# A hybrid decoder layer on one core: orders of VectorE, GpSimd and LayerNorm work in the projection and the MLP, and later places for GLA's and RG-LRU's matmuls

## Chip, core and metric

The kernel runs on one core of a Trainium2 chip. The metric is the device time of one execution in microseconds. TensorE multiplies matrices (PE in the rows), VectorE (DVE), ScalarE (ACT) and GpSimd (POOL) work element by element, and SyncE (SP) issues the DMAs. Each engine has a list of instructions of its own and takes it strictly in order; an instruction whose input or buffer isn't ready holds up everything behind it in that list. Engines are joined by semaphores.

## What is computed

One post-LayerNorm decoder layer over 2048 tokens of width 1024, in float32:

```python
def _layer_norm(x, g, b):  # mean and variance over the 1024 columns, eps 1e-5
    ...
# each layer:
z   = h @ w_in                       # one projection, its columns shared among three mixers
#   S5     : diagonal complex state space, 16 groups x 16 channels, GLU (width 256)
#   GLA    : gated linear attention in chunks of 64, 4 heads (width 512)
#   RG-LRU : causal convolution of width 4, gates, a real linear recurrence (width 256)
mix = concat(S5, GLA, RG-LRU) @ w_out
h   = LayerNorm(alpha * h + mix)
h   = LayerNorm(alpha * h + relu(h @ mlp_w1)^2 @ mlp_w2)   # hidden width 4096
```

Ahead of the layer the input goes through a LayerNorm too.

## The kernel before

**Products.** Every float32 product is done as three TensorE matmuls of rounded halves (`mm3`, L226 to L228), so a weight or activation has to be split into a high and a low half first: ScalarE copies the rounded half, VectorE subtracts it (`split`, L1373 and the helper line L75). All VectorE and GpSimd instructions are recorded on L75, since they go through a counting wrapper there.

**Stages.** From 0 to about 680 us the input projection and the three mixers; to about 890 us the output projection with LayerNorm 1 and the transposes of its result; to about 1545 us the first MLP product; to about 2235 us the second; and a tail with LayerNorm 2.

**How the order is made.** The program writes each engine's list itself. Up to the output projection there is a plan of ticks, each a group of some 12 or 24 matmuls; in each tick `step()` is called twice and moves every generator in `active` on to its next `yield`. So a `yield` puts what follows half a tick later in every engine's list. One GLA unit (`gla_unit`) is such a generator: it makes decayed queries and keys (`gla_qz`, `gla_kz`) on VectorE, then the scores (`gps`) and a transpose of the keys (`kt`), the state update (`up`), the states (`gs`, VectorE), the output (`ov`) and its transpose (`ot`). `lru_work` is one generator over 8 units: convolution (`xc`), two gate products (`lps`), then sigmoids, scan and output. Besides, `filler` and other generators are taken on while the cost counted for VectorE or GpSimd in the tick is under a budget.

**Output projection.** `out_tile(i, dh)` makes one half of a 128-token tile (`po`) and adds it to the residual `acc`. `ln1_work` is one generator that takes the 16 tiles one after another, `tj_work` one that transposes the finished rows in 32 groups of four 128x128 blocks (`tjp`, PSUM), empties each into a `tjo` tile of seven operands of a fast matrix product (two copies by ScalarE, two differences by VectorE, two by GpSimd, two buffers) and stores it to `rop_d`. The first MLP product loads these operands back as `act` and `ring` pieces.

**MLP.** Both products use a Strassen-Winograd scheme: seven products p1, p2, p7, p6, p3, p4, p5 (`ORDER`) in three PSUM banks a, b, c. The first has 32 steps of seven products of 12 matmuls, the second 64 parts of seven products of 6. `run` goes through all of them with a counter n, one per product; p3 of a step is done in the next step at its place. Besides the products, each position n has a list of tasks put there by number: `task(n, fn)`. What is left of the transposes and the ring pieces when the first product begins is done by `tail_step`, two half-steps at each of the positions 0 to 10. `steps[n].hsum` makes the squared hidden activations out of the products. `Chunk` loads and adds up blocks of w2 (`load`, `sum`, `split`); `Part.evac` adds the seven products onto the quarters c11, c12, c21, c22 of an accumulator `accq`, on VectorE straight out of PSUM (`pa_m`, `pb_m`, `pc_m`), on GpSimd out of copies that ScalarE made (`p_m`, `u_m`, three rotating buffers of `pu_tile`). In the last eight parts `Acc.ln` and `Acc.ln_apply` do LayerNorm 2 of the two rows of a tile: statistics on VectorE, a power on GpSimd, then scale on ScalarE, the gain product on VectorE and the shift half on VectorE, half on GpSimd (`gb`).

## Time and profile before

| | us |
|---|---|
| median of three runs | 2258.49 |
| the three runs | 2260.07, 2258.49, 2255.2 |
| the profiled execution, as reported | 2259.39 |
| its span, first to last instruction | 2257.7 |

The profile is of one execution. A wait is idle time of an engine right ahead of an instruction, put down to what ended last of what it waited for. The granted clock is that of TensorE as a share of its full speed, averaged over a stretch. Matmuls are pipelined: one of 512 columns is shown as 0.39 us, while the next starts 0.227 us later.

### The profile page before, as it was taken

The numbers are of one execution on the slowest core, as the hardware profiler recorded it, in microseconds if no ns is written. First come the engines' busy times: TensorE is split into PE (matmuls) and PEld (weight loads), VectorE is DVE, ScalarE is ACT, GpSimd is POOL, SyncE is SP. The second block draws the span as 40 slices with busy tenths as digits, with TensorE's granted clock in tenths as the row PEclk, the third lists the DMA queues.
The fourth block names the chain that finished last, engine by engine and source line by source line (L and its number), as shares of the span: only waits on it lengthen the run. The fifth ranks groups of instructions, "written<-read, shape, count | busy, mean of one in ns | idle before, by whom it ended". The sixth has DMA issues, their size and how long they took to land. (4 is left out here: it accounts for less than half of the span.)

```text
span 2257.7 us, 29781 instructions
## 1 busy us (share of the span) xinstructions
PE 2067.0 (92%) x9920; PEld 1712.9 (76%) x9920; DVE 1584.5 (70%) x2262; ACT 1027.0 (45%) x2045; POOL 1147.3 (51%) x1087
## 2 busy tenths in 40 slices
PE   6977999899999998799999999998999999999863
PEld 6866779888987776588887888886788888888652
DVE  6567865546547556677778877776688888888887
ACT  3336655657663222333334433334544545444431
POOL 5486630000003444466666666666566675667554
PEclk9998999999999999899999999999999999999976
DMA  7342354455354676544447444437544344434332
GB/s 212 102 129 74 98 167 137 121 138 140 99 177 131 175 232 204 146 150 153 150 154 256 151 153 154 148 128 266 185 131 135 94 134 131 135 98 134 111 105 77
DMA packets 378457, 328.24 MB, mean 145 GB/s; under 512 B 72240, under 2 KB 314560, under 8 KB 378304
## 3 DMA queue, kind: packets, MB, share of 16 engines
q1 hardware_dynamic: 377536, 324.24, 46.5%
q0 software_dynamic: 768, 2.11, 0.4%
q8 instruction: 78, 1.28, 0.2%
q14 instruction: 75, 0.61, 0.1%
HBM read 208.23 MB, written 118.63 MB: 145 GB/s over the span
## 5 line engine op out<-in xcount | busy, mean ns | idle before, releaser
L75 DVE TENSOR_TENSOR ho_m<-ho_m 128x512 fp32r<-128x512 f32 (+1 forms) x256 | 259.3, 1038 | 68.2 <-ACT ho_m L1373 55.9
L75 POOL TENSOR_TENSOR accq<-accq,p_m 128x512 f32<-128x512 f32 x128 | 199.9, 1579 | 200.4 <-DVE accq L75 155.9
L75 POOL TENSOR_TENSOR cp<-cp,cp 128x512 f32<-128x512 f32 x128 | 196.0, 1540 | 183.2 <-ACT cp L1562 180.6
L75 DVE TENSOR_TENSOR w1o_s<-w_s,w1o_s 128x512 fp32r<-128x512 f32 x160 | 208.6, 1318 | 46.6 <-ACT w1o_s L1373 46.5
L75 POOL TENSOR_TENSOR ss<-ss,cst 128x4 f32<-128x4 f32 x16 | 17.6, 1102 | 365.8 <-DVE ss L75 365.8
L227 PE MATMUL pa_m<-act,ho_m 128*128 128x512 f32 x384 | 150.4, 392 | 2.0 <-DVE act L75 1.9
L226 PE MATMUL pa_m<-act,ho_m 128*128 128x512 f32 x384 | 150.3, 391 | 2.0 <-ACT p_m L1792 1.4
L228 PE MATMUL pa_m<-act,ho_m 128*128 128x512 f32 x384 | 150.1, 391 | 1.2 <-DVE ho_m L75 1.2
L1373 ACT ACTIVATE ho_m<-ho_m 128x512 fp32r<-128x512 f32 (+1 forms) x256 | 135.6, 569 | 30.7 <-DMA ho_m<-hid_d 30.7
L1373 ACT ACTIVATE w1o_s<-w_s 128x512 fp32r<-128x512 f32 x160 | 99.9, 626 | 103.1 <-PE pb_s L228 51.8
L1792 ACT ACTIVATE p_m<-pa_m 128x512 f32<-128x512 f32 x64 | 38.3, 599 | 221.7 <-PE pa_m L228 216.0
L226 PE MATMUL pa_s<-ring,w1o_s 128*128 128x512 f32 x256 | 103.0, 402 | 11.0 <-ACT ring L1373 6.3
L226 PE MATMUL pc_m<-act,ho_m 128*128 128x512 f32 x256 | 102.4, 400 | 5.5 <-ACT p_m L1792 5.4
L226 PE MATMUL po<-act,w_mx 128*128 128x512 f32 x256 | 106.9, 418 | 0.1
L75 POOL TENSOR_TENSOR accq<-accq,u_m 128x512 f32<-128x512 f32 x64 | 106.2, 1659 | 0.6 <-ACT u_m L1792 0.6
L75 DVE SCALAR_TENSOR_TENSOR cp<-cp 128x512 f32<-128x512 f32 x96 | 101.9, 1061 | 3.3
L227 PE MATMUL pa_s<-ring,w1o_s 128*128 128x512 f32 x256 | 102.2, 399 | 1.9 <-DVE ring L75 1.9
L228 PE MATMUL po<-act,w_mx 128*128 128x512 f32 x256 | 103.2, 403 | 0.9 <-DVE w_mx L75 0.9
L227 PE MATMUL pc_s<-act,w1o_s 128*128 128x512 f32 x256 | 101.4, 396 | 1.8 <-DVE act L75 1.8
L227 PE MATMUL po<-act,w_mx 128*128 128x512 f32 x256 | 102.8, 402 | 0.0
L226 PE MATMUL pc_s<-act,w1o_s 128*128 128x512 f32 x256 | 102.6, 401 | 0.0
L228 PE MATMUL pc_m<-act,ho_m 128*128 128x512 f32 x256 | 101.5, 397 | 0.5 <-DVE ho_m L75 0.5
(437 smaller groups left out, 6553.3 us busy)
## 6 DMA issues: line engine op xcount, KB each, us to landing
hid_d<-cp SPq DMA_DIRECT2D x224, 256.0 KB, 2.3
ho_m<-hid_d SPq DMA_DIRECT2D x384, 128.0 KB, 2.3
w_s<-in_mlp_w_dram SPq DMA_DIRECT2D x32, 1024.0 KB, 5.7
w<-in_mlp_w_dram SPq DMA_DIRECT2D x16, 1024.0 KB, 7.0
rop_d<-tjo SPq DMA_DIRECT2D x32, 448.0 KB, 4.6
w<-s5w_d SPq DMA_DIRECT2D x16, 640.0 KB, 5.1
xr<-in_x_dram SPq DMA_DIRECT2D x16, 512.0 KB, 4.9
h_d<-xr SPq DMA_DIRECT2D x16, 512.0 KB, 4.4
```

What stands on the lines that cost most here:

```text
L75: return fn(*a, **k)
L226: T.matmul(ps, lhs[0], rhs[0], start=first, stop=False, skip_group_check=more)
L227: T.matmul(ps, lhs[0], rhs[1], start=False, stop=False, skip_group_check=more)
L228: T.matmul(ps, lhs[1], rhs[0], start=False, stop=last, skip_group_check=more)
L1373: S.activation(dst_hi, src, COPY)
L1792: S.activation(t, ps, COPY)
```

## The change

Five places.

1. RG-LRU's generator yields twice more at the end of a unit, GLA's twice more between the keys and the scores and once more ahead of the output.
2. LayerNorm 1 is one generator for each tile, put into `active` when the tile's second half is added, in place of one generator over all. A transpose group takes one more half-step, and each pair of rows waits for both.
3. First MLP product: `tail_step` goes to position 17, the last ring piece is split two half-steps later, p3 of step 0 is done in step 2 just ahead of p7, and the tasks that hang on it move along (`hsum`, one split).
4. First chunk of w2: its first half is loaded five positions earlier and its two first sums are made half by half, from position L0 on in place of L0 + 2. In `evac`, GpSimd adds u2 behind VectorE's p4 and p7 behind VectorE's p5, in place of ahead of them; the copies stay where they were.
5. LayerNorm 2: row 1 at position 10 and row 0 at 13 in place of 0 at 13 and 1 at 14, each applied two positions later in place of two and three.

```diff
@@ lru_work, end of a unit
                     late.append(bind(mix_store, 6 + ct, b * BLK, gi))
+                    yield
+                    yield
@@ gla_unit, ahead of gps; ahead of ov
-        for _ in range(3):
+        for _ in range(5):
             yield
...
         gstate[hp] = st
+        yield
         yield
@@ out_tile, ln1_work, tj_work
             if dh:
-                z["acc", i] = True
+                active.append(ln1_work(i))
...
             if j == 0:
+                while ("row", 2 * g) not in z:
+                    yield
                 yield
                 yield
...
                 late.append(bind(z.__setitem__, ("tj", g), True))
+            yield
             yield
@@ run
-                who = prev if p == "p3" else g
...
+                if p != "p3":
+                    who = [(g, p)]
+                    if at_ == 2 and p == "p7":
+                        who.insert(0, (groups[0], "p3"))
+                else:
+                    who = [(groups[at_ - 1], p)] if at_ > 1 else []
@@ tail and tasks of the first product
-        for _ in range(4):
+        for _ in range(6):
             yield
...
-    for n in range(11):
+    for n in range(18):
         task(n, tail_step)
         task(n, tail_step)
...
-        for w, k in ((1, 5), (3, 6), (2, 6), (4, 7)):
+        for w, k in ((1, 10), (3, 10), (2, 11), (4, 11)) if n == 0 else ((1, 5), (3, 6), (2, 6), (4, 7)):
@@ Part.evac
             elif p == "p7":
-                self.add("c22", G, self.copy(bank["c"], "p7"))
+                self.p7 = self.copy(bank["c"], "p7")
             elif p == "p6":
-                self.add("c21", G, self.copy(bank["a"], "u2"))
+                self.u2 = self.copy(bank["a"], "u2")
             elif p == "p4":
                 self.add("c21", V, bank["c"])
+                self.add("c21", G, self.u2)
             elif p == "p5":
                 self.add("c22", V, bank["a"])
+                self.add("c22", G, self.p7)
@@ first chunk of w2; LayerNorm 2
-    task(L0, chunks[0].load)
-    for k, w in ((2, 3), (3, 1), (4, 2), (6, 4)):
+    task(L0 - 5, chunks[0].load, 0)
+    task(L0, chunks[0].load, 1)
+    for k, w, j in ((0, 3, 0), (1, 1, 0), (2, 3, 1), (3, 1, 1)):
+        task(L0 + k, chunks[0].sum, w, (j,))
+    for k, w in ((4, 2), (6, 4)):
         task(L0 + k, chunks[0].sum, w)
...
-        for i, k in ((0, 13), (1, 14)):
+        for i, k in ((1, 10), (0, 13)):
             task(n + k, acc[g].ln, i)
-            task(n + k + 2 + i, acc[g].ln_apply, i)
+            task(n + k + 2, acc[g].ln_apply, i)
```

ScalarE's list in the mixers, where the gate of a GLA unit (`gc`), the convolution of an RG-LRU unit (`xc`) and the copy of a projected RG-LRU gate (`lg`) meet. Before:

```order
L782 ACTIVATE gc_0_0_1969<-gc_0_0_1969 128x256
L783 ACTIVATE gc_0_0_1969<-gc_0_0_1969,cst 128x256
L724 ACTIVATE xc_0_1982<-xl_0_1921,lcb,lcw 128x512
L1024 ACT_TABLE_LOAD
L1024 ACTIVATE lg_0_2006<-pz_lg_1_1944 128x512
L791 ACT_TABLE_LOAD
```

And now:

```order
L784 ACTIVATE gc_0_0_1970<-gc_0_0_1970 128x256
L785 ACTIVATE gc_0_0_1970<-gc_0_0_1970,cst 128x256
L1027 ACT_TABLE_LOAD
L1027 ACTIVATE lg_0_2002<-pz_lg_1_1949 128x512
L793 ACT_TABLE_LOAD
L793 ACTIVATE gc_0_0_1970<-ga_0_0_1968 128x256
L794 ACTIVATE gd_0_0_1971<-ga_0_0_1968 128x256
L795 ACTIVATE gb_0_0_1969<-gb_0_0_1969 128x256
L797 ACTIVATE dec_0_0_2013<-ga_0_0_1968 128x4
L724 ACTIVATE xc_0_2020<-xl_0_1926,lcb,lcw 128x512
```

`xc` of the next RG-LRU unit stood ahead of `lg` and now stands behind it and behind the four exponentials of the GLA gate.

VectorE's list at the start of the first MLP product, around the last LayerNorm row (the two `acc_8204` operations), the weight splits (`w1o_s`) and the emptying of a transpose group (`tjo`). Before:

```order
L75 TENSOR_TENSOR tjo_8578<-tjp_8556,tjo_8578 128x128
L75 TENSOR_TENSOR tjo_8578<-tjo_8578,tjp_8556 128x128
L75 SCALAR_TENSOR_TENSOR acc_8204<-acc_8204,mv_ln_15_8541,g_ln_6662 128x640
L75 TENSOR_TENSOR w1o_s_5_8595<-s_s_7810,w1o_s_5_8595 128x512
L75 TENSOR_TENSOR act<-act 128x2x512 x2
L75 TENSOR_TENSOR w1o_s_0_8607<-w_s_7924,w1o_s_0_8607 128x512
L75 TENSOR_TENSOR w1o_s_1_8610<-w_s_7924,w1o_s_1_8610 128x512
L75 TENSOR_TENSOR w1o_s_2_8614<-w_s_7924,w1o_s_2_8614 128x512
L75 SCALAR_TENSOR_TENSOR acc_8204<-acc_8204,rs_ln_15_8543,b_ln_6663 128x640
L75 TENSOR_TENSOR tjo_8632<-tjp_8590,tjo_8632 128x128
L75 TENSOR_TENSOR tjo_8632<-tjo_8632,tjp_8590 128x128
```

And now:

```order
L75 SCALAR_TENSOR_TENSOR acc_8204<-acc_8204,mv_ln_15_8513,g_ln_6652 128x640
L75 TENSOR_TENSOR cp_8573<-pb_s_8528,p_s_8541 128x512
L75 SCALAR_TENSOR_TENSOR cp_8573<-cp_8573 128x512
L75 SCALAR_TENSOR_TENSOR acc_8204<-acc_8204,rs_ln_15_8515,b_ln_6653 128x640
L75 TENSOR_TENSOR w1o_s_5_8584<-s_s_7805,w1o_s_5_8584 128x512
L75 TENSOR_TENSOR act<-act 128x2x512 x2
L75 TENSOR_TENSOR w1o_s_0_8596<-w_s_7921,w1o_s_0_8596 128x512
L75 TENSOR_TENSOR w1o_s_1_8599<-w_s_7921,w1o_s_1_8599 128x512
L75 TENSOR_TENSOR w1o_s_2_8603<-w_s_7921,w1o_s_2_8603 128x512
L75 TENSOR_TENSOR tjo_8620<-tjp_8579,tjo_8620 128x128
L75 TENSOR_TENSOR tjo_8620<-tjo_8620,tjp_8579 128x128
```

The second half of the LayerNorm row stood behind the splits of `w1o_s` 5, 0, 1 and 2 and now stands ahead of them; the emptying of the group that followed it stands right behind the splits.

VectorE's list in the tail, one part: the first `pc_m` addition is c21 of a part, the statistics (`BN_STATS` to the short `rs`) are a LayerNorm row, `ho_m` are splits for the next part, `gb` the gain product and the shift. Before, from c21 of one part on:

```order
L75 TENSOR_TENSOR accq_13324<-accq_13324,pc_m_18268 128x512
L75 BN_STATS st_1_0_18333<-accq_13194 128x6 x2
L75 BN_AGGR mv_1_0_18336<-st_1_0_18333 128x2
L75 TENSOR_SCALAR rs_1_0_18338<-mv_1_0_18336 128x1
L75 SCALAR_TENSOR_TENSOR rs_1_0_18338<-mv_1_0_18336,rs_1_0_18338 128x1
L75 TENSOR_TENSOR accq_13324<-accq_13324,pa_m_18234 128x512
L75 BN_STATS st_1_1_18350<-accq_13194 128x6 x2
L75 BN_AGGR mv_1_1_18353<-st_1_1_18350 128x2
L75 TENSOR_SCALAR rs_1_1_18355<-mv_1_1_18353 128x1
L75 SCALAR_TENSOR_TENSOR rs_1_1_18355<-mv_1_1_18353,rs_1_1_18355 128x1
L75 TENSOR_TENSOR ho_m_0_18281<-ho_m_0_18281 128x512
L75 TENSOR_TENSOR accq_13194<-accq_13194,gb_18163 128x1024
```

And now:

```order
L75 TENSOR_TENSOR accq_13324<-accq_13324,pc_m_18274 128x512
L75 BN_STATS st_1_0_18347<-accq_13195 128x6 x2
L75 BN_AGGR mv_1_0_18350<-st_1_0_18347 128x2
L75 TENSOR_SCALAR rs_1_0_18352<-mv_1_0_18350 128x1
L75 SCALAR_TENSOR_TENSOR rs_1_0_18352<-mv_1_0_18350,rs_1_0_18352 128x1
L75 TENSOR_TENSOR accq_13324<-accq_13324,pa_m_18248 128x512
L75 TENSOR_TENSOR ho_m_0_18287<-ho_m_0_18287 128x512
L75 TENSOR_TENSOR accq_13195<-accq_13195,gb_18163 128x1024
L75 TENSOR_TENSOR accq_13195<-accq_13195,gb_18163 128x512
L75 TENSOR_TENSOR accq_13324<-accq_13324,pb_m_18365 128x512
L75 TENSOR_TENSOR ho_m_3_18327<-ho_m_3_18327 128x256
L75 TENSOR_TENSOR ho_m_1_18317<-ho_m_1_18317 128x512
```

The second row's statistics (`st_1_1`) followed on the first's with one addition between; now one row's statistics stand behind c21, and the next tile's other row (`st_2_1`) follows only after a split, the gain product, the shift, an addition and two splits.

## Rows read from the trace of the kernel before

**Rows 1.** The page: busy us (share of the span) and instructions of each engine
```profile
PE 2067.0 (92%) x9920; PEld 1712.9 (76%) x9920; DVE 1584.5 (70%) x2262; ACT 1027.0 (45%) x2045; POOL 1147.3 (51%) x1087
```

**Rows 2.** TensorE's waits, whole span: us in total, times, longest
```profile
PE pa_m L226 <- DVE accq L75: 44.1, 14, 9.7
...
PE gps L810 <- DVE gla_kz L75: 9.3, 5, 2.8
...
PE ov L842 <- DVE gs L75: 7.3, 1, 7.3
PE pr_v L226 <- ACT lg L1024: 6.4, 1, 6.4
...
PE lps L732 <- DVE xc L75: 2.9, 1, 2.9
```

**Rows 3.** Stretches: length, busy us (instructions) of PE, PEld, DVE, ACT, POOL; clock
```profile
60.00:300.00 240.00, 202.64 (x1105) 169.05 (x1104) 165.97 (x324) 124.37 (x279) 158.44 (x331) 0.92 0.37 107
...
690.00:890.00 200.00, 180.79 (x834) 146.56 (x832) 123.25 (x229) 55.30 (x138) 92.55 (x126) 0.96 0.62 188
890.00:960.00 70.00, 51.09 (x193) 39.83 (x194) 45.60 (x60) 26.07 (x51) 35.20 (x37) 0.80 0.56 168
...
1610.00:2105.00 495.00, 492.31 (x2165) 405.78 (x2165) 408.78 (x500) 238.04 (x457) 318.32 (x207) 1.00 0.41 122
2105.00:2258.00 153.00, 89.84 (x332) 69.74 (x331) 123.37 (x182) 46.95 (x70) 75.43 (x56) 0.78 0.31 97
```

**Rows 4.** ScalarE, timeline around lg: start, us, instruction, idle before
```profile
188.01 0.51 ACT L783 ACTIVATE gc<-gc,cst 128x256 f32<-128x256 f32 x1
191.68 0.81 ACT L724 ACTIVATE xc<-xl,lcb,lcw 128x512 f32<-128x512 f32 x1 [3.16 <-DVE lgi L75]
...
193.93 0.60 ACT L1024 ACTIVATE lg<-pz_lg 128x512 f32<-128x512 f32 x1
```

**Rows 5.** VectorE, timeline in the first GLA unit
```profile
126.05 1.28 DVE L75 SCALAR_TENSOR_TENSOR xr<-xr,rs_in,b_in 128x1024 f32<-128x1024 f32 x1 [6.70 <-POOL rs_in L75]
...
130.33 0.28 DVE L75 COPY gs<-up 128x128 f32<-128x128 f32 x1
```

**Rows 6.** Waits from 690 to 890 us, of TensorE and of ScalarE
```profile
PE tjp L1320 <- DVE tjo L75: 11.6, 6, 3.9
PE tjp L1320 <- DVE acc L75: 4.4, 2, 4.1
...
ACT tjo L1324 <- DMA rop_d<-tjo: 52.0, 9, 6.8
```

**Rows 7.** TensorE's waits from 890 to 960 us
```profile
PE tjp L1320 <- DVE tjo L75: 8.9, 1, 8.9
PE pa_s L226 <- ACT ring L1373: 6.3, 1, 6.3
PE pa_s L226 <- DVE tjo L75: 4.7, 1, 4.7
```

**Rows 8.** ScalarE, timeline at the last ring piece
```profile
943.41 1.06 ACT L1373 ACTIVATE ring<-ring 128x1024 fp32r<-128x1024 f32 x1 [5.40 <-DMA ring<-rop_d]
```

**Rows 9.** GpSimd, timeline at the first chunk of w2; then a stretch
```profile
1533.86 1.29 POOL L75 TENSOR_TENSOR t<-w 128x512 f32<-128x512 f32 x1 [8.00 <-DMA w<-in_mlp_w_dram]
...
1540.00:1556.00 16.00, 10.42 (x36) 6.26 (x34) 15.96 (x12) 11.76 (x21) 15.38 (x10) 0.95 0.63 206
```

**Rows 10.** VectorE, timeline of the tail
```profile
2141.22 0.69 DVE L75 TENSOR_TENSOR accq<-accq,pc_m 128x512 f32<-128x512 f32 x1 [0.56 <-POOL accq L75]
...
2191.45 1.78 DVE L75 TENSOR_TENSOR ho_m<-ho_m 128x512 fp32r<-128x512 f32 x1
...
2200.65 0.69 DVE L75 TENSOR_TENSOR ho_m<-ho_m 128x512 fp32r<-128x512 f32 x1
...
2228.03 0.69 DVE L75 TENSOR_TENSOR accq<-accq,pc_m 128x512 f32<-128x512 f32 x1 [1.78 <-POOL accq L75]
```

**Rows 11.** The page, costliest groups: busy, mean ns, idle before and releaser
```profile
L75 POOL TENSOR_TENSOR accq<-accq,u_m 128x512 f32<-128x512 f32 x64 | 106.2, 1659 | 0.6 <-ACT u_m L1792 0.6
```

More of the change, by code (lines that the diff above doesn't have):

```diff
@@ L1286, in out_tile, with ln1_work @@
             tick([un], bind(pe, h, un), ev if h else None)
-    def ln1_work():
-        for i in range(NT):
-            while ("acc", i) not in z:
-                yield
-            g = ln_steps(accs[i], z["gb1"], f"ln1_{i}", 384)
-            next(g)
-            yield
-            yield
-            yield
-            for _ in g:
-                yield
-            late.append(bind(lambda i: store(h1_d[i * P:i * P + P, :], accs[i]), i))
-            yield
-            z["row", i] = True
+    def ln1_work(i):
+        g = ln_steps(accs[i], z["gb1"], f"ln1_{i}", 384)
+        next(g)
+        yield
+        yield
+        yield
+        for _ in g:
+            yield
+        late.append(bind(lambda i: store(h1_d[i * P:i * P + P, :], accs[i]), i))
+        z["row", i] = True
     def set_gb(key, g_ap, b_ap, nm):
@@ L1313, in tj_work @@
             if j == 0:
+                while ("row", 2 * g) not in z:
+                    yield
                 yield
@@ L1333, in tj_work @@
                 late.append(bind(z.__setitem__, ("tj", g), True))
+            yield
             yield
@@ L1438, in evac @@
             last = None
-        for g in groups:
+        for at_, g in enumerate(groups):
             for p in ORDER:
-                who = prev if p == "p3" else g
-                if who is not None:
-                    products(who, p)
-                evac()
-                if who is not None:
-                    last = who, p
+                if p != "p3":
[4 more added lines that the diff above has]
+                    who = [(groups[at_ - 1], p)] if at_ > 1 else []
+                for w in who:
+                    products(*w)
+                    evac()
+                    last = w
+                if not who:
+                    evac()
                 for e in tasks.pop(n, ()):
@@ L1647, in hymba_layer_kernel @@
         task(b + max(2, o), m.sum, 4)
-        for i, k in ((2, 2), (3, 3), (4, 4), (5, 6), (6, 6)):
+        for i, k in ((2, 2), (3, 3), (4, 4), (5, 6), (6, 11 if n == 1 else 6)):
             task(b + max(k, o), m.split, i)
@@ L1665, in __init__, with load, sum @@
             self.c = c
-            self.op = [None] * 7
-        def load(self):
-            self.b = {}
-            for j in range(2):
-                r = raw_tile([P, 2, D], f"w2_{self.c}_{j}")
-                k = 4 * self.c + 2 * j
-                load(r, w2_v[:, k:k + 2, :])
-                self.b.update({("11", j): r[:, 0, 0:512], ("12", j): r[:, 0, 512:D],
-                               ("21", j): r[:, 1, 0:512], ("22", j): r[:, 1, 512:D]})
-        def sum(self, which):
+            self.op, self.b = [None] * 7, {}
+        def load(self, j):
+            r = raw_tile([P, 2, D], f"w2_{self.c}_{j}")
+            k = 4 * self.c + 2 * j
+            load(r, w2_v[:, k:k + 2, :])
+            self.b.update({("11", j): r[:, 0, 0:512], ("12", j): r[:, 0, 512:D],
+                           ("21", j): r[:, 1, 0:512], ("22", j): r[:, 1, 512:D]})
+        def sum(self, which, js=(0, 1)):
             b = self.b
-            for j in range(2):
+            for j in js:
                 if which in (2, 3):
@@ L1850, in hymba_layer_kernel @@
             task(b + 6, chunks[c].split, 6)
-        task(b + 9, ch.load)
+        for j in range(2):
+            task(b + 9, ch.load, j)
         for k, w in ((15, 3), (22, 1), (33, 2), (40, 4)):
@@ L2034, in hymba_layer_kernel @@
                 z["tj bank"] = lambda i, shp, nm: psum("tp", shp, nm)
-                active.append(ln1_work())
                 active.append(tj_work())
```

## The prediction

> **What bounds the kernel now.** I read the page's busy line first, then the waits of TensorE, then the stretches. TensorE is busy 2067.0 of 2257.7 us [rows 1]; in the long middle of the second MLP product it is busy 492.31 of 495 us at clock 1.00 [rows 3]. So most of the span is matmul time that no reordering touches, and the change can only win what TensorE loses: its waits [rows 2] and the matmuls that run at a lower granted clock after them. The stretches say where: 60 to 300 us (clock 0.92), 690 to 890 (0.96), 890 to 960 (51.09 busy of 70, clock 0.80), and 2105 to the end (89.84 busy of 153) [rows 3]. A window at a mean of 0.96 between the two levels of 1.2 and 2.4 GHz has spent about 8% of its time at the lower: of 200 us that is 16 us, in which half the work is done, so about 8 us lost on top of the waits. I call that the clock loss.
>
> The profiled execution spans 2257.7 us and is reported as 2259.39; the sum below is taken from the latter. The median of the three runs is 2258.49, 0.9 below it, so the two may be used for one another.
>
> **Mixers (the added yields of RG-LRU and GLA), forecast -10.** A GLA unit's score matmuls (gps) wait for DVE's kz 9.3 us in five waits, the longest 2.8 [rows 2]. The two extra steps put twelve projection matmuls ahead of them, at 0.227 us each 2.7 us: the waits nearly vanish. The RG-LRU yields act through ACT. At 188.52 ACT has ended the log of a GLA gate; next in its list stands xc of the next RG-LRU unit, for which it sits idle 3.16 us until DVE lets go of the buffer; only behind that comes the copy of lg, ended at 194.53 [rows 4], and TensorE waits 6.4 us for the bank that it empties [rows 2]. In the changed list lg stands ahead of xc: table load 1.28 and copy 0.60 from 188.6 on end it at 190.5, which is 4 us earlier. The wait of lps for xc (2.9 [rows 2]) loses the same 2.7 us of lead: -2.7.
>
> Against this stands the first GLA unit. DVE idles 6.70 us until 126.05 because GpSimd's power for a LayerNorm row stands behind a long list of small S5 operations, and gs (130.33) follows that; TensorE's ov waits 7.3 us for gs [rows 2, 5]. GpSimd's list there is unchanged, so 126.05 holds. But in the changed DVE list the masked copy of the scores stands behind that stalled row instead of ahead of it, and gs behind a further LayerNorm row. From 126.05 the S5 rows take the same 4.3 us to 130.33 [rows 5], and the masked copy, the statistics and first half of that LayerNorm row and a few small ones some 5 us more, so gs comes at about 135.5. TensorE gets there at the same 123.3 as now (130.6 - 7.3), since the first gps wait of 2.7 is gone and twelve matmuls more lie ahead. It then loses 12.2 us where gps and ov together lost 10.0: +2.2, a wait made longer by the edit. Sum: -6.6 (the four other gps waits, 9.3 - 2.7) + 2.2 - 4 - 2.7 = -11.1, with some clock loss less and some waits that only move on. I take -10. Bounds: nothing of it won and the later GLA and RG-LRU ends costing 3, to all the waits and 6 of clock: +3 to -18.
>
> **Out-projection (one LayerNorm generator a tile, a third step a transpose group), forecast -15.** Here the transposes (tjp, one PSUM bank) wait for DVE to empty the last group 11.6 us in six waits, and 4.4 us for LayerNorm's acc [rows 6]: 16 us, and 8 of clock, so 24 to be won. DVE's copies wait for ACT's, and ACT waits 52.0 us for stores of earlier groups (rop_d<-tjo, two buffers) [rows 6]. One more step makes a group 1.5 ticks, 4.1 us, where it was 2.7, which gives a copy 1.4 us more before the next group asks. With one LayerNorm generator a tile the rows no longer queue behind one another, so acc should be ready sooner. ACT's wait for stores is not cured by order: it is a rate, two buffers for each store's landing. Since it is mostly hidden (52 us of ACT for 12 of TensorE) and each group now brings 1.4 us more cover, I take 60% of 24, -15. Bounds: 0 (the stores' rate decides) and -24.
>
> **Start of the first MLP product, forecast -9.** TensorE waits 4.7 us for a copy, 8.9 us in front of group 28's transposes, and 6.3 us for the last ring piece [rows 7]. The first is untouched. In the second, DVE's copy stands behind three weight splits and the second half of the last LayerNorm row (1.9 us); in the changed list that half stands ahead of the splits, so -2. In the third, product p3 of step 0 needs a ring piece whose load lands late: ACT idles 5.40 us for it and copies its first half from 943.41 to 944.47 [rows 8]. With the second half and the matmuls at the lower clock behind the wait (mean 0.80 in this stretch [rows 3]) I put the 6.3 us at about 10. The change moves this p3 from position 11 to just ahead of position 16's p7, five products or some 13.6 us later, while the split is two half-steps later and the transposes before it are spread out further. The loads then need to be at most 6 us later than now to be fully hidden; I take 7 of the 10. Together -9, bounds -3 and -13.
>
> **Second MLP's first chunk, forecast -4.** GpSimd waits 8.0 us for the first half-chunk of w2 and starts its sum at 1533.86 [rows 9]; DVE's splits then pile up, and TensorE is busy 10.42 of the 16 us from 1540 to 1556 [rows 9], in small waits. The first half's load moves five products (13.6 us) up and its sums by two, so the pile should be gone at its head; the second half stays. -4, bounds -1 and -6. The 5.4 us wait around 1589 behind the next chunk's loads is not touched.
>
> **Evacuation in the second MLP, forecast 0.** u2 and p7 are now added by GpSimd after DVE's adds instead of before. TensorE is full here [rows 3], so nothing is to be won until the tail. DVE need no longer wait for GpSimd at c21 and c22; in return three rotating copy buffers are held longer.
>
> **Tail, forecast -10.** From 2114 on LayerNorm 2 makes DVE the bound: c21's adds start at 2141.22 and five parts later at 2228.03 [rows 10], 17.6 to 17.8 us a part (15.9 the last), where matmuls alone need 42 x 0.227 = 9.5. TensorE's accq waits of 44.1 us [rows 2] lie mostly here. A period is twelve DVE pieces: four PSUM adds of 0.60, two LayerNorm rows of 2.52 with their 0.73 waits for a power, three and a half splits, two gain products and two shift adds. Unhindered they sum to 13.2 us. The rest is hindrance: a split of two SBUF operands takes 1.78 us where the same form takes 0.69 [rows 10]: it runs while GpSimd adds, and ends with it. The Trainium skill says why, in "GPSIMD Engine Reference", section 1, Specifications: GpSimd's SBUF interfaces are shared with VectorE, in contention when a DVE instruction has two SBUF inputs. The trace agrees, PSUM adds not being slowed; with the rule alone, and GpSimd always apart, a period would be the 13.2.
>
> In the new order GpSimd's u2 and p7 adds come later in a period, DVE loses the wait of 0.56 ahead of c21 [rows 10], and one row's LayerNorm stands between adds instead of both in a run. Laying both lists side by side, with each two-input operation that meets a GpSimd add ending with it, I get 16.3 us a period, not 17.7: -1.45 in each of five. The last interval is 14.1, not 15.9: -1.8. From c21's last add to the end it is 29.7 now (2257.7 - 2228.03); with row 1 done first, and one row left for the very end, I lay 25.6: -4.1. Row 1 of the first tile is now ahead in the interval before: +2.5. Together -10.6; I take -10, bounds -3 (hindrance moved, not removed) and -15.
>
> **The sum.** 2259.4 - 10 - 15 - 9 - 4 - 0 - 10 = 2211. Clock losses that fall with the waits are in the terms.
>
> **Rivals.** (a) Waits that move on. The transposes are limited by store rate (52.0 us of ACT [rows 6]), the mixers' queues by GpSimd's list [rows 5], and removing one wait uncovers the next: projection 0, mixers -2, start -4, chunk -2, tail -6, hence 2245. For it speaks that ACT's wait is four times TensorE's; against it, that each group gets 1.4 us of cover. (b) Slower: GpSimd's adds hold the copy buffers. GpSimd's add of u takes 1.66 us [rows 11]. If the late adds end after ACT needs the buffer again, TensorE's bank a is emptied late in every part. Three buffers for three copies a part: it decides once u2's add ends after the next part's p1 has been evacuated. Then 56 full parts lose about one add less the slack, 1 us each, +56, and against the -48 the time is 2267. Against it: GpSimd is busy about two thirds of the period there and its queue was early, 0.6 us of waiting before all 64 adds [rows 11], though that also means that it runs close behind ACT. (c) No change within 0.2%: only if two of the three large terms fail and a new wait appears, 2258. That the change does nothing is excluded by the lists, which differ at each of these places.
>
> **Chances.** Forecast (2195 to 2228) 0.62; (a) around 2245 0.22; (c) 0.05; (b) 0.11. Faster by over 0.2% (4.5 us, about what a measurement can tell from no change) is then 0.84, within it 0.05, slower 0.11. The terms' bounds add to -4 to -76, which don't all go one way; cutting the slower cases and the top of (a), the range is 2193 to 2244.
>
> **What the changed profile would show.** gps waits gone, lg's wait near 2 us, ov's wait longer (about 12 us, near 123 to 135). In 690 to 960 fewer tjp waits and a clock nearer 1; no ring wait of several us. Between 1535 and 1556 fewer small gaps. In the tail c21's adds 16.3 us apart, and 25 to 26 us from the last to the end. Wrong would be: the same sum of tjp waits under other groups; ACT waiting for GpSimd before its copies in the second MLP; c21's adds still 17.7 apart.

## The result

| | median us | before in the same job | ratio, 95% interval |
|---|---|---|---|
| changed kernel | 2221.7 | 2257.84 | 0.9843 [0.9826, 0.986] |

The change makes the kernel 1.6% faster, 36 us; the forecast of 2211 is 47 below this median of the kernel before. The profiled execution's span went from 2257.7 to 2223.7 us, -34.0.

To see where the time went I made a ledger out of the two traces. Both kernels issue the same 9920 matmuls of the same sizes. At full speed one of 512 columns starts 0.2265 us behind the last. I count a narrower one in proportion, and all of them add up to 1877.9 us of work. What the clock shows beyond the work done so far I call lost: waiting, matmuls at the lower clock, and what some matmuls, narrow ones above all, take beyond that count at any time (those of 128 columns start 0.11 us apart in both traces, counted as 0.057). The last of these is about 100 us of each sum below, 88 of them up to 500 us of work, by an estimate from the median spacing of each group; it is the same in both kernels, so only differences between kernels are read here. In each stretch of work the two kernels can be compared, though their times have shifted:

```
us lost, by work done (us):   0-500  500-650  650-750  750-1250  1250-1300  1300-1800  1800-end   sum
before                        189.6     38.8     34.2      13.5       20.5        5.2      77.9  379.8
changed                       202.2     18.8     22.1      13.5       21.2        2.9      65.2  345.8
difference                    +12.6    -20.0    -12.1       0.0       +0.7       -2.3     -12.7  -34.0
forecast                        -10      -15       -9         0         -4          0       -10    -48
                             mixers  project.   MLP 1                chunk      MLP 2      tail
```

(The sums are of the parts before rounding.) The chunk won nothing, and the mixers, where 10 us were to be won, lost 12.6; the other stretches did as forecast or better.

The changed kernel's waits of TensorE over the whole span (us in total, times, longest) answer to [rows 2]:

```profile
PE pa_m L226 <- DVE accq L75: 27.6, 8, 7.8
PE ov L845 <- DVE gs L75: 12.8, 3, 6.4
PE tjp L1321 <- DVE tjo L75: 10.5, 4, 8.1
...
PE pr_v L226 <- ACT lg L1027: 8.2, 2, 6.7
PE ov L843 <- DVE gla_sc L75: 8.2, 1, 8.2
...
PE gps L812 <- DVE gla_kz L75: 1.0, 1, 1.0
```

gps fell from 9.3 to 1.0 as forecast, and accq from 44.1 to 27.6; but ov waits 21.0 us in all (12.8 for states, 8.2 for masked scores) in place of 7.3, and lg did not fall. The stretches (length, busy of PE, PEld, DVE, ACT, POOL; clock), for [rows 3]; the same us hold somewhat different work:

```profile
60.00:300.00 240.00, 206.39 (x1122) 171.77 (x1121) 165.87 (x332) 126.73 (x285) 157.48 (x332) 0.91 0.37 108
300.00:690.00 390.00, 368.45 (x2240) 323.20 (x2241) 200.20 (x442) 245.51 (x548) 13.81 (x17) 0.97 0.49 135
690.00:890.00 200.00, 190.05 (x903) 155.85 (x902) 141.45 (x250) 63.70 (x158) 100.38 (x135) 0.98 0.67 202
890.00:960.00 70.00, 60.58 (x266) 48.87 (x265) 49.70 (x61) 30.75 (x58) 38.85 (x34) 0.93 0.54 160
...
1610.00:2105.00 495.00, 494.61 (x2174) 407.30 (x2174) 435.58 (x515) 234.30 (x454) 293.77 (x204) 1.00 0.41 123
```

From 690 to 890 TensorE is busy 190.05 us where it was 180.79, and from 890 to 960 it is 60.58 where it was 51.09, at clock 0.93 in place of 0.80. From 300 to 690 it is down to 368.45 from the 379.01 of the kernel before:

```profile
300.00:690.00 390.00, 379.01 (x2314) 331.21 (x2313) 209.66 (x464) 254.18 (x566) 16.04 (x18) 0.99 0.50 136
```

### The profile page after: what moved, and what is told of

Read it like the earlier page. It is cut to its first block, busy times and chain, and to the rows that moved or that the text cites. A ratio compares the mean times of both kernels' runs of the same rounds, so it can differ in the third digit from the quotient of the medians.

```text
span 2223.7 us, 29800 instructions
## 1 busy us (share of the span) xinstructions
PE 2062.0 (93%) x9920; PEld 1710.0 (77%) x9920; DVE 1602.4 (72%) x2262; ACT 1023.9 (46%) x2046; POOL 1123.1 (51%) x1087
## 3 DMA queue, kind: packets, MB, share of 16 engines
q8 instruction: 78, 1.28, 0.3%
## 5 line engine op out<-in xcount | busy, mean ns | idle before, releaser
L75 DVE TENSOR_TENSOR ho_m<-ho_m 128x512 fp32r<-128x512 f32 (+1 forms) x256 | 280.7, 1126 | 63.2 <-ACT ho_m L1375 40.6
L75 POOL TENSOR_TENSOR accq<-accq,p_m 128x512 f32<-128x512 f32 x128 | 185.7, 1457 | 70.0 <-DVE accq L75 59.5
L75 POOL TENSOR_TENSOR accq<-accq,u_m 128x512 f32<-128x512 f32 x64 | 87.0, 1359 | 159.3 <-DVE accq L75 141.2
L226 PE MATMUL pc_m<-act,ho_m 128*128 128x512 f32 x256 | 104.1, 406 | 7.4 <-ACT p_m L1798 6.9
L226 PE MATMUL po<-act,w_mx 128*128 128x512 f32 x256 | 104.3, 408 | 0.0
L228 PE MATMUL po<-act,w_mx 128*128 128x512 f32 x256 | 101.4, 396 | 1.1 <-DVE w_mx L75 1.1
L228 PE MATMUL pc_m<-act,ho_m 128*128 128x512 f32 x256 | 101.8, 398 | 0.5 <-DVE ho_m L75 0.5
L227 PE MATMUL pc_m<-act,ho_m 128*128 128x512 f32 x256 | 102.0, 399 | 0.0
```

Of the source, the lines that this page charges most:

```text
L75: return fn(*a, **k)
L226: T.matmul(ps, lhs[0], rhs[0], start=first, stop=False, skip_group_check=more)
L227: T.matmul(ps, lhs[0], rhs[1], start=False, stop=False, skip_group_check=more)
L228: T.matmul(ps, lhs[1], rhs[0], start=False, stop=last, skip_group_check=more)
```

## The experiments

Medians of four executions each. The kernel before ran in each job beside them, so the ratios are what compares (the changed kernel: 0.9843).

| kernel | median us | before in its job | ratio, 95% interval |
|---|---|---|---|
| no_mixer_yields | 2209.78 | 2254.24 | 0.9800 [0.9786, 0.9815] |
| lru_yields_only | 2215.85 | 2254.24 | 0.9832 [0.9817, 0.9846] |
| no_gps_yields | 2205.59 | 2254.24 | 0.9785 [0.9769, 0.9802] |
| before_plus_mixer_yields | 2263.47 | 2254.24 | 1.0041 [1.0026, 1.0056] |
| projection_undone | 2235.96 | 2256.69 | 0.9916 [0.9900, 0.9931] |
| no_transpose_yield | 2228.80 | 2256.69 | 0.9880 [0.9866, 0.9895] |
| mlp_start_undone | 2240.73 | 2256.69 | 0.9938 [0.9921, 0.9955] |
| ln2_order_undone | 2219.18 | 2256.69 | 0.9839 [0.9824, 0.9853] |
| late_adds_undone | 2226.70 | 2253.72 | 0.9883 [0.9869, 0.9898] |
| first_chunk_undone | 2225.26 | 2253.72 | 0.9876 [0.9859, 0.9894] |
| no_gps_yields_ln2_old | 2203.99 | 2253.72 | 0.9780 [0.9764, 0.9796] |
| ov_yield_only_ln2_old | 2208.44 | 2253.72 | 0.9796 [0.9782, 0.9811] |

And what their ledgers say, in us lost:

```
                          0-500  500-650  650-700  1250-1300  1300-1800  1800-end
before                    189.6     38.8     33.9       20.5        5.2      77.9
changed                   202.2     18.8     21.7       21.2        2.9      65.2
no_mixer_yields           190.3     16.2     22.3       19.7        2.9      65.2
lru_yields_only           196.8     16.0     21.8       18.7        2.8      65.2
no_gps_yields             185.9     17.8     22.0       19.0        2.8      65.2
before_plus_mixer_yields  199.9     34.6     30.4       21.3        5.2      77.8
projection_undone         199.6     34.6     20.7       20.6        2.8      65.2
no_transpose_yield        199.9     29.1     18.1       19.0        2.9      65.2
mlp_start_undone          198.1     30.6     29.8       19.1        2.9      65.2
ln2_order_undone          200.2     18.9     21.8       18.5        2.8      63.6
late_adds_undone          197.4     18.3     21.9       19.5        5.2      70.4
first_chunk_undone        202.7     18.5     21.4       22.6        2.9      65.2
no_gps_yields_ln2_old     186.9     17.2     21.1       19.4        2.8      63.5
ov_yield_only_ln2_old     191.0     17.1     22.2       18.9        2.9      63.6
```

Where two kernels don't differ in a stretch their entries show the spread of a single execution: up to 5 us in the mixers (197.4 to 202.7 in seven executions of the changed mixers, 200.0 in the mean), 0.6 in the projection (18.3 to 18.9 in the four with the same mixers and projection), under 3 in the chunk's stretch, 0.2 or less in the late ones.

### What the mixers lose, 12.6 us here and about 10 in the mean

**no_mixer_yields**: all five added yields out.

```diff
-                    yield
-                    yield
...
-        for _ in range(5):
+        for _ in range(3):
...
         gstate[hp] = st
-        yield
         yield
```

> The changed kernel with all five added yields of the mixers (RG-LRU's two, GLA's two ahead of gps and one ahead of ov) taken out again; the rest of the change stays. Matmul by matmul, the time that TensorE loses against its own full-speed spacing up to 500 us of work (about where GLA ends) is 189.7 us before and 202.1 us after. Theory A, the yields cost those 12.4 us: loss there back to about 190 and 2222 - 12 = 2210 us. Rival B, the later GLA is what makes room in the projection (loss from 500 to 650 us of work 38.7 before, 18.7 after): the loss up to 500 falls by 12, that from 500 to 650 rises by about as much, 2220 us.

2209.78 us, ratio 0.9800. The loss up to 500 is 190.3, that of before, and the projection's stays low at 16.2. Theory A holds and rival B falls: the later GLA isn't what makes room in the projection.

**before_plus_mixer_yields**: the kernel before and nothing but those five yields.

```diff
                     late.append(bind(mix_store, 6 + ct, b * BLK, gi))
+                    yield
+                    yield
...
-        for _ in range(3):
+        for _ in range(5):
...
         gstate[hp] = st
+        yield
         yield
```

> The kernel before with nothing but the five yields of the mixers added. Theory A, they cost 12.4 us whatever follows: 2258 + 12 = 2270 us. Rival B, they pay in the projection: 2250 to 2258 us.

It is 0.41% slower than before, some 9 us, nearer theory A's 12 than rival B's gain. The mixers lose 10.3 more, and the old projection gets 4.2 back (34.6 for 38.8). So a first part of rival B is there with the old projection, but it does not pay for the mixers.

**lru_yields_only**: GLA's three yields out, RG-LRU's two in.

```diff
-        for _ in range(5):
+        for _ in range(3):
...
         gstate[hp] = st
-        yield
         yield
```

> The changed kernel with GLA's three added yields taken out; RG-LRU's two stay. Theory A1, GLA's yields cost the time, through states and masked scores that now stand behind stalled work in VectorE's list: about 2210 us, ov's waits back to 7.3 us in all from 21.0. Rival A2, RG-LRU's yields cost it: about 2222 us.

2215.85 us, ratio 0.9832, near the changed kernel's 0.9843; its profiled span, 2213.1, is 10.6 us less. Neither number of the two theories was met. RG-LRU's yields are not harmless by themselves: 196.8 against 190.3. The waits of TensorE from 60 to 720 us:

```profile
PE gps L812 <- DVE gla_kz L75: 12.0, 6, 4.9
PE ov L844 <- DVE gs L75: 6.8, 3, 5.6
...
PE s_xtp L672 <- DVE s_x L75: 5.6, 2, 4.1
PE s_xtp L676 <- DVE s_w L75: 4.5, 4, 1.3
PE ytp L986 <- ACT sg L1001: 4.2, 3, 1.7
```

ov is at 6.8, which GLA's yields had at 21.0, as theory A1 has it. But a new wait stands at ytp (4.2), and gps and s_xtp are no lower than before. Presumably work that RG-LRU's unit did at one place now meets S5's and GLA's at another; no run shows which.

**no_gps_yields**: the two yields ahead of gps out, the others in.

```diff
         z["gla_qk", i] = True
-        for _ in range(5):
+        for _ in range(3):
```

> The changed kernel without the two yields ahead of gps; the one ahead of ov and RG-LRU's two stay. If the loss comes from the masked copy and the states sliding behind the stalled LayerNorm row and behind the weights of the output projection, which the two gps yields do, about 2212 us with gps waits back at about 9 us. If it is the yield ahead of ov, about 2220 us.

2205.59 us, ratio 0.9785, clear of the changed kernel and below the 2212 expected; it is also faster than no_mixer_yields by the medians of one job, though the intervals overlap. With the other three in place the two gps yields cost some 13.6 us (200.0, the changed mixers' mean, to 186.4, the mean of this and no_gps_yields_ln2_old). Its waits of TensorE from 60 to 720:

```profile
PE gps L812 <- DVE gla_kz L75: 9.1, 5, 3.0
PE pr_v L226 <- ACT lg L1027: 6.4, 1, 6.4
PE ov L845 <- DVE gs L75: 6.2, 2, 5.6
```

gps is back at 9.1, and ov down from 21.0 to 6.2. So the two yields took 8 us out of one wait and put 15 into the next one.

**ov_yield_only_ln2_old** and **no_gps_yields_ln2_old** (below) differ only in RG-LRU's two yields.

The second of them is no_gps_yields with LayerNorm 2's old order, the first that and

```diff
                     late.append(bind(mix_store, 6 + ct, b * BLK, gi))
-                    yield
-                    yield
```

> The same with RG-LRU's two yields taken out too, so that of the mixers' yields only the one ahead of ov is left. With none of the five the mixers lost 190 us up to 500 us of work, with RG-LRU's and ov's 186. If ov's yield wins it, 2203 us or less here; if RG-LRU's do, 2208 us.

2208.44 against 2203.99, in the mixers 191.0 against 186.9: the number expected if RG-LRU's yields win it. But they don't win it by themselves. With ov's yield alone the mixers stand where they stood with none (190.3); with RG-LRU's alone they are worse (196.8); with both they are better by some 4 us. That is near the spread of a single ledger, and the intervals of the two ratios overlap, so the sign of it is likely and the size is not shown.

### Projection and start of the first product

**projection_undone**: one LayerNorm generator over all tiles and two steps a transpose group, as before.

```diff
-                active.append(ln1_work(i))
+                z["acc", i] = True
...
-    def ln1_work(i):
+    def ln1_work():
+        for i in range(NT):
+            while ("acc", i) not in z:
+                yield
...
             if j == 0:
-                while ("row", 2 * g) not in z:
-                    yield
...
-            yield
             yield
...
+                active.append(ln1_work())
                 active.append(tj_work())
```

> The changed kernel with the output projection as before: one LayerNorm generator over all tiles, two steps a transpose group. What TensorE loses between 500 and 650 us of work is 38.8 us before and 18.8 after. Theory A, these edits alone win it: 2222 + 20 = 2242 us. Rival B, it only moves stalls into or out of the first MLP steps (650 to 700 us of work, 33.9 before, 21.7 after): 500 to 650 rises by 20, 650 to 700 falls by some 8, 2234 us.

2235.96, ratio 0.9916. The projection's loss goes from 18.8 to 34.6, +15.8; nothing comes back later (20.7 for 21.7), so rival B falls, though the time is nearer its 2234 than theory A's 2242. The missing 4.2 to before's 38.8 are those that before_plus_mixer_yields showed, whose ledger in this stretch is the same 34.6. Without the mixers' yields the same edits win more, 22.6 (38.8 in the kernel before, 16.2 in no_mixer_yields). tjp's wait from 690 to 960 us:

```profile
PE tjp L1323 <- DVE tjo L75: 21.8, 8, 8.7
```

**no_transpose_yield**: only the third step of a transpose group out.

```diff
                 late.append(bind(z.__setitem__, ("tj", g), True))
             yield
-            yield
```

> The changed kernel without the added yield of a transpose group alone; one LayerNorm generator a tile stays. If the third step is what lets VectorE empty a group in time, tjp waits go back to about 11 us in the projection and the time to 2236 us or so; if the LayerNorm generators do it, 2222 to 2226 us. I expect two thirds from the yield: 2235 us.

2228.80, ratio 0.9880. The projection loses 29.1: of its 15.8 us the yield gives 10.3, the LayerNorm generators and the wait for both rows 5.5. The two thirds were right, the time (2235) not, since the first product starts better without it (18.1 for 21.7), and tjp's wait for tjo, 7.3, is short of the 11 expected. Waits of TensorE from 690 to 960:

```profile
PE tjp L1321 <- DVE tjo L75: 7.3, 7, 2.2
PE tjp L1321 <- ACT w1o_s L1374: 5.8, 1, 5.8
...
PE tjp L1321 <- DVE acc L75: 3.9, 2, 2.0
```

**mlp_start_undone**: p3 of step 0, the task positions, `hsum` and the ring piece's yields as before, and the transpose generator as before.

```diff
...
-                    if at_ == 2 and p == "p7":
-                        who.insert(0, (groups[0], "p3"))
...
+                who = prev if p == "p3" else g
...
-        for _ in range(6):
+        for _ in range(4):
             yield
...
-    for n in range(18):
+    for n in range(11):
...
-            yield
             yield
```

> The changed kernel with the start of the first MLP product as before (p3 of step 0 in step 1, 11 positions of half-steps, hsum and split tasks as before) and, since the slower transposes need those positions, the transpose generator as before too. To be read from the loss between 650 and 700 us of work: with the moved p3 as the cause of its gain it goes from 21.7 back to about 34, with the ring wait of some 6 us; with the transposes' spacing as the cause it stays near 22 in this kernel's sibling without the transpose yield and the ring wait doesn't return. Time by the first about 2222 + 12 + 13 = 2247, by the second 2235 us.

2240.73. Against no_transpose_yield the stretch from 650 to 700 rises from 18.1 to 29.8, and the ring wait is back:

```profile
PE pa_s L226 <- ACT ring L1372: 6.9, 1, 6.9
```

So the edits at the start of the product are together worth 11.7 us, as the first expectation had it; the time lies between the 2247 and 2235 named. That the ring wait is back points at the moved p3, but no run parts it from its tasks and the two half-steps. (The sibling also has the pair of rows waited for; its projection differs by 1.5.)

### Tail and chunk

**ln2_order_undone**: LayerNorm 2's tasks at their old positions, GpSimd's late adds kept.

```diff
-        for i, k in ((1, 10), (0, 13)):
+        for i, k in ((0, 13), (1, 14)):
             task(n + k, acc[g].ln, i)
-            task(n + k + 2, acc[g].ln_apply, i)
+            task(n + k + 2 + i, acc[g].ln_apply, i)
```

> The changed kernel with LayerNorm 2's tasks at their old positions; GpSimd's late adds stay. The tail's loss (from 1800 us of work on) is 77.9 us before and 65.2 after, a period of c21's adds 17.7 and 16.1. Theory A, the order of the rows gives most of it, the end above all (29.7 to 25.7 us behind c21's last add): loss 76, 2232 us, period 17.4. Rival B, GpSimd's late adds give the shorter period, the row order only the end: loss 70, 2227 us, period 16.5.

Both were wrong. The tail loses 63.6, less than the changed kernel's 65.2; the time, 0.9839, can't be told from 0.9843. VectorE's c21 adds in this kernel:

```profile
2142.73 0.67 DVE L75 TENSOR_TENSOR accq<-accq,pc_m 128x512 f32<-128x512 f32 x1
...
2158.74 0.67 DVE L75 TENSOR_TENSOR accq<-accq,pc_m 128x512 f32<-128x512 f32 x1
...
2174.75 0.67 DVE L75 TENSOR_TENSOR accq<-accq,pc_m 128x512 f32<-128x512 f32 x1
...
2187.80 0.68 DVE L75 TENSOR_TENSOR accq<-accq,pc_m 128x512 f32<-128x512 f32 x1
```

The period is 16.0 us with the old row order, and the end behind the last add is the old 29.7 (2217.5 - 2187.80), but the last interval is 13.05.

**late_adds_undone**: the other way round, GpSimd's adds back ahead of VectorE's, the new row order kept.

```diff
             elif p == "p7":
-                self.p7 = self.copy(bank["c"], "p7")
+                self.add("c22", G, self.copy(bank["c"], "p7"))
             elif p == "p6":
-                self.u2 = self.copy(bank["a"], "u2")
+                self.add("c21", G, self.copy(bank["a"], "u2"))
...
-                self.add("c21", G, self.u2)
...
-                self.add("c22", G, self.p7)
```

> The changed kernel with GpSimd's adds of u2 and p7 back ahead of VectorE's; LayerNorm 2 keeps its new order. With the row order undone the tail lost 63.6 us, as little as in the changed kernel (65.2; before 77.9), period 16.0. Theory A, the late adds alone carry the tail's gain: loss about 78, period 17.6, small accq waits of some 2 us in all back in the middle of the second product, 2222 + 15 = 2237 us. Rival B, either order is enough by itself: loss about 66, 2224 us.

Loss 70.4, in between. VectorE's c21 adds here:

```profile
2150.53 0.68 DVE L75 TENSOR_TENSOR accq<-accq,pc_m 128x512 f32<-128x512 f32 x1
...
2166.88 0.68 DVE L75 TENSOR_TENSOR accq<-accq,pc_m 128x512 f32<-128x512 f32 x1
...
2183.23 0.68 DVE L75 TENSOR_TENSOR accq<-accq,pc_m 128x512 f32<-128x512 f32 x1
```

The period is 16.35, and the middle of the second product loses 5.2 as before. So each order by itself brings the period from 17.7 to 16.0 or 16.35. In the tail the late adds alone win 14.3, the row order alone 7.5, both together 12.7. The row order has nothing left to win once the adds are late.

**first_chunk_undone**: both halves of the first w2 chunk at L0 and the sums from L0 + 2.

```diff
-    task(L0 - 5, chunks[0].load, 0)
+    task(L0, chunks[0].load, 0)
     task(L0, chunks[0].load, 1)
-    for k, w, j in ((0, 3, 0), (1, 1, 0), (2, 3, 1), (3, 1, 1)):
-        task(L0 + k, chunks[0].sum, w, (j,))
-    for k, w in ((4, 2), (6, 4)):
+    for k, w in ((2, 3), (3, 1), (4, 2), (6, 4)):
```

> The changed kernel with the first chunk of w2 as before: both halves loaded at L0, sums from L0 + 2. The changed trace has GpSimd waiting 6.6 us for the second half in place of 8.0 for the first, and VectorE's pile as before. If the second half sets the pile, the loss between 1250 and 1300 us of work stays at 18.5 to 21.3 us, the spread of the kernels so far, time 2222 us. If the early half helps after all, 2224 to 2226 us.

Its stretch loses 22.6, more than any kernel with the edit (18.5 to 21.2); the two others without it, both built on the kernel before, lost 20.5 and 21.3. The edit is then worth some 2 us, at the size of the spread; the time's interval touches the changed kernel's. Loss and time (2225.26) are where the expectation put them if the early half helps after all; that it wins half of the forecast's 4 is likely and not shown.

### A version faster than both

**no_gps_yields_ln2_old**: the changed kernel without the two gps yields and with LayerNorm 2's old order.

```diff
-        for _ in range(5):
+        for _ in range(3):
...
-        for i, k in ((1, 10), (0, 13)):
+        for i, k in ((0, 13), (1, 14)):
...
-            task(n + k + 2, acc[g].ln_apply, i)
+            task(n + k + 2 + i, acc[g].ln_apply, i)
```

> The changed kernel without the two gps yields and with LayerNorm 2's old order: both made the changed kernel slower. If the two add, 2205.6 - 2 = 2204 us, faster than either kernel; the tail's loss 63.6.

2203.99 us, ratio 0.9780 [0.9764, 0.9796]: the fastest, clear of the changed kernel (0.9843) and the kernel before. Most of that is the gps yields; against no_gps_yields (0.9785) the old row order can't be told from none in time, though the tail's loss is the expected 63.5.

## Why the prediction was right and where it was wrong

The time lies in the range and in the forecast's own band. The sum of -48 is too large by 14 us of the span's -34, and what made it so is one term: the mixers, whose measured +12.6 (about 10 in the mean) lies outside the bounds given (+3 to -18). The rest was forecast at -38 and measured at -46.6. That the time stayed within the band is in part luck: the mixers missed by 22.6 us, and the other terms, which won 8.6 more than forecast, made up for some of it. Rival (a), waits that move on, came true in the mixers alone.

**Mixers: four steps, of which two held.** *gps* lost its waits, as worked out, and the wait of *lps* for xc (2.9) is gone. *lg* was to end at 190.5, 4 us earlier, because xc no longer stands ahead of it. ScalarE in the changed kernel:

```profile
188.21 0.51 ACT L785 ACTIVATE gc<-gc,cst 128x256 f32<-128x256 f32 x1
194.29 1.28 ACT L1027 ACT_TABLE_LOAD   x1 [5.57 <-DVE lgi L75]
195.58 0.60 ACT L1027 ACTIVATE lg<-pz_lg 128x512 f32<-128x512 f32 x1
```

lg does stand ahead of xc now, and waits 5.57 us by itself, for VectorE's product lgi of the last unit with its lg: ScalarE may write the new lg only when the old one has been read. The kernel before, VectorE and then ScalarE:

```profile
190.36 1.28 DVE L75 TENSOR_TENSOR_SCAN lgi<-lr,lru_carry,xc 128x512 f32<-128x512 f32 x1
...
191.86 0.69 DVE L75 TENSOR_TENSOR lgi<-lgi,lg 128x512 f32<-128x512 f32 x1
...
192.63 1.28 ACT L1024 ACT_TABLE_LOAD   x1
```

There xc had waited for another lgi, the scan, which reads the last xc and ended at 191.64; the product ended at 192.55, and lg's table load began at 192.63. So with xc out of its way lg had 0.1 us to win, not 4. The idle time in [rows 4] was in front of xc, and I took it for the only wait there. The step that failed is "in the changed list lg stands ahead of xc: ... from 188.6 on". I should have asked what lg itself waits for, since the wait of the instruction in front had hidden its own.

*ov* was forecast to lose 12.2 us in the first unit with gps. It lost 8.2 + 2.4, at the place and for the reason given (gs came at 134.7, forecast 135.5):

```profile
131.07 1.20 PE L843 MATMUL ov<-v,gla_sc 128*128 128x128 f32 x4 [8.23 <-DVE gla_sc L75]
134.67 0.58 PE L845 MATMUL ov<-gs,gla_qz 128*128 128x128 f32 x1 [2.41 <-DVE gs L75]
...
173.44 0.80 PE L845 MATMUL ov<-gs,gla_qz 128*128 128x128 f32 x2 [3.97 <-DVE gs L75]
```

What I didn't do is to ask the same of the other 15 GLA units. At 173 the second unit's states stand behind a LayerNorm row and S5's set-up (4.0 us), and at 685 they stand behind the split of an output-projection weight (VectorE, then ScalarE):

```profile
683.98 1.23 DVE L75 TENSOR_TENSOR act<-wo,act 128x1024 fp32r<-128x1024 f32 x1 [8.36 <-ACT act L1130]
685.12 1.49 DVE L75 SCALAR_TENSOR_TENSOR gs<-gs,dec,up 128x128 f32<-128x128 f32 x4
...
682.89 1.06 ACT L1130 ACTIVATE act<-wo 128x1024 fp32r<-128x1024 f32 x1 [9.65 <-DMA wo<-in_w_out_dram]
```

ScalarE idles 9.65 us for the load of wo, VectorE 8.36 for ScalarE, and the states of a GLA unit, which have all they need, wait behind: 6.4 us of TensorE. In VectorE's list without the gps yields the same states stand ahead of that split. So the failing step is "The two extra steps put twelve projection matmuls ahead of them", taken as cover and nothing else. A later place gives cover against what is late in VectorE's work for that unit; it also takes the unit's next VectorE work past whatever stands in the list in between, and some of that waits for a DMA or for GpSimd. no_gps_yields and before_plus_mixer_yields show it from both sides. Two more waits of TensorE rose that the forecast doesn't name: py from 5.9 to 10.1 us in all, and pz_lg, which had none, to 3.9; pz_lg's are gone again in no_gps_yields.

Of the 12.6 us some 7 are idle time and some 5 matmuls issued below full speed, if the two traces are split by whether TensorE stood still: longer waits bring the clock loss with them, which the bounds counted on the winning side alone.

**Projection: right, at the lower end in size.** -15 was forecast for these edits; they win 15.8 with the mixers' yields (projection_undone) and 22.6 without them (no_mixer_yields). The mixers' yields win 4.2 by themselves in the old projection and cost 2.6 in the new one (18.8 for 16.2), so the two edits don't add up, which was not foreseen. tjp waits from 690 to 890 us fell as forecast, to 2.1 and 1.8 from 4.4 and 11.6 [rows 6], and ScalarE's wait for stores was indeed mostly hidden.

**Start of the first product: right.** -9 forecast, -12.1 in the ledger, 11.7 for all its edits by mlp_start_undone. The ring wait of 6.3 [rows 7] is gone but for 0.8 us on a split by VectorE. The wait for group 28 was to shrink by 2 and shrank from 8.9 to 8.1; the 4.7 is untouched.

**First chunk: wrong in its mechanism.** The changed kernel, GpSimd and then VectorE:

```profile
1506.02 1.75 POOL L75 TENSOR_TENSOR t<-w 128x512 f32<-128x512 f32 x1
...
1516.12 1.29 POOL L75 TENSOR_TENSOR t<-w 128x512 f32<-128x512 f32 x1 [6.64 <-DMA w<-in_mlp_w_dram]
...
1519.26 3.49 DVE L75 TENSOR_TENSOR act<-w,act 128x512 fp32r<-128x512 f32 x2
1522.67 1.78 DVE L75 TENSOR_TENSOR ho_m<-ho_m 128x512 fp32r<-128x512 f32 x1
```

The first half is there in time, its sum done at 1507.8. But GpSimd waits 6.64 us for the second half, where the kernel before waited 8.00 for the first [rows 9] and 2.54 more for the second, and the pile of VectorE's splits begins only then. "The second half stays" was written and its consequence wasn't drawn: a product needs both halves.

**Second product: 0 forecast, -2.3.** The small accq waits there are gone, and late_adds_undone brings them back (5.2 for 2.9). Rival (b), copy buffers held too long, did not happen: a few new waits for p_m, 0.6 to 1.4 us each, show in the tail alone, also in late_adds_undone and not in ln2_order_undone, so they come with the row order.

**Tail: right in size, wrong in its cause.** VectorE's c21 adds, for [rows 10]:

```profile
2151.86 0.68 DVE L75 TENSOR_TENSOR accq<-accq,pc_m 128x512 f32<-128x512 f32 x1
...
2167.95 0.68 DVE L75 TENSOR_TENSOR accq<-accq,pc_m 128x512 f32<-128x512 f32 x1
...
2184.02 0.68 DVE L75 TENSOR_TENSOR accq<-accq,pc_m 128x512 f32<-128x512 f32 x1
...
2197.98 0.68 DVE L75 TENSOR_TENSOR accq<-accq,pc_m 128x512 f32<-128x512 f32 x1
```

The period is 16.1 (forecast 16.3), the last interval 13.96 (14.1), the end 25.7 (25.6), the loss 12.7 less (10). The layout side by side of the two lists held to a few tenths. One reading in it was a little off: a slowed split doesn't end with GpSimd's add. The one of 1.78 us [rows 10] ends at 2193.23, the add that it ran beside at 2192.68. But "in the new order" put down to both edits, and in the forecast's accounts to the row order, what the late adds alone would have given; the two experiments part them, and the row order's shorter end is paid for in the first interval between c21 adds of the tail: 13.0 us in the changed kernel (from 2090.66), 8.8 in ln2_order_undone (from 2086.09).

## What to carry to other kernels

A wait in an in-order list that is cured by moving its consumer back can return larger elsewhere (here gps 8 us down, ov 14 up): look up for the moved instruction, and for all that its unit issues behind it, what each would itself wait for, and what it is moved behind; do it for every unit, not for the one whose wait is the longest. When an instruction in front of it is waiting, an instruction's own wait is not in the trace. And when two edits aim at one stall, undo each of them by itself, since both may cure it and one may then be a burden.

## What the runs showed of the hardware

Operations of two SBUF inputs slow each other on both engines, down to short ones. In the changed kernel GpSimd works on S5's tables from 187 to 194 us, where it had nothing to do before. VectorE beside it, in the GLA and RG-LRU chain:

```profile
189.51 1.10 DVE L75 TENSOR_TENSOR_SCAN ga<-cmask,gb 128x256 f32<-128x256 f32 x1
...
191.62 1.53 DVE L75 TENSOR_TENSOR_SCAN lgi<-lr,lru_carry,xc 128x512 f32<-128x512 f32 x1
...
193.37 0.84 DVE L75 TENSOR_TENSOR lgi<-lgi,lg 128x512 f32<-128x512 f32 x1
```

The first of them in the kernel before (the two others stand above, beside lg):

```profile
189.05 0.69 DVE L75 TENSOR_TENSOR_SCAN ga<-cmask,gb 128x256 f32<-128x256 f32 x1
```

and GpSimd in the changed kernel:

```profile
187.97 0.62 POOL L75 TENSOR_TENSOR s_p<-s_la,s_lb 128x256 f32<-128x256 f32 x1
...
189.27 0.79 POOL L75 TENSOR_TENSOR s_tab<-s_p,s_q 128x256 f32<-128x256 f32 x1
190.13 0.90 POOL L75 TENSOR_TENSOR s_p<-s_la,s_lb 128x256 f32<-128x256 f32 x1
...
192.14 1.52 POOL L75 TENSOR_TENSOR s_tab<-s_p,s_q 128x256 f32<-128x256 f32 x1
```

Both lists show them side by side. The scan of 256 takes 1.10 us where the same one took 0.69 in the kernel before, that of 512 1.53 (1.28), the product 0.84 (0.69); GpSimd's product s_p of 256 takes 0.62 at 187.97, while VectorE stands idle, and 0.90 beside it; its sums s_tab, of one form, take 0.79 and 1.52. The Trainium skill names the shared interfaces in "GPSIMD Engine Reference", section 1, Specifications; the trace agrees and gives the sizes. I had expected this of the long adds of the second product, not of a mixer's short steps. The chain that lg waits for ends at 194.2, before at 192.6; it began 0.2 us later, so 1.5 us are such slowing.
